# A decoder trunk on one core: first stage with filling products and a dummy activation ahead of x, smaller first pieces, and the sums of squares and small vectors behind the transposed x

## The chip, the core and the metric

The kernel runs on one core of a Trainium2 chip. A core has TensorE (PE, the matrix products; PEld is its weight load), VectorE (DVE), ScalarE (ACT), GpSimd (POOL) and SyncE (SP, which here only issues loads), each with an instruction queue of its own that it works off in order, and sixteen DMA engines that all queues share. Time is device time of one launch in microseconds (us). A profiled execution gives start and length of every instruction.

## What is computed

Two decoder layers on `x` of 256 tokens by 2048 features, float32. Only the head of the first one is touched: an RMS norm, scaled by `mix_norm[0]`, and the product with `conv_w_in` (2048 by 4096).

```python
def rms_norm(x, g):
    y = xf * lax.rsqrt(jnp.mean(xf * xf, axis=-1, keepdims=True) + EPS)
    return y * g
def conv_module(h, w_in, b_in, dw, ...):
    u = h @ w_in + b_in
    a, gate = jnp.split(u, 2, axis=-1)
    v = a * jax.nn.sigmoid(gate)
    v = lax.conv_general_dilated(v, dw[:, None, :], ..., feature_group_count=D_MODEL) + dw_b
    ...
    return v @ w_out + b_out
x = x + conv_module(rms_norm(x, mix_norm[0]), ...)
x = x + mlp(rms_norm(x, mlp_norm[0]), w_up, w_down)
...                                   # second layer: state-space mixer and mlp, then a final norm
```

## The kernel before

Weights are read once from HBM in **steps** of 1 MB, in order (`load`, through `fetch`, on SP's queue; three buffers `raw`). A step is used in two **halves**. For each half `split` makes two matrices: `hi`, the weight rounded by an ACT copy, and `lo`, weight minus `hi`, a subtraction on DVE or, from step 4 on, on POOL (four buffers each). PE then forms hi x hi, hi x lo and lo x hi.

The first product runs over 16 **blocks** of output columns. A block has two steps, so four halves (block 0: halves 0 to 3, block 1: halves 4 to 7, block 2: halves 8 to 11), and a half has 24 products (`mm_g`, L202 to L204) into an `acc` buffer, of which there are two. The right-hand side is the transposed and `mix_norm`-scaled x, `hT`, in 16 feature groups hT0 to hT15, each with a rounded part (ACT, L249) and a rest (DVE, L250), from transposes by PE (L245, tile `xt`), two groups to a PSUM bank.

The norm's factor per token is not applied to x. Sums of squares (`sumsq`: ACT L262 and DVE L259, 128x512 each) give `ss`, `ssm`, then `rstd` by a power on POOL (L277); `bcast_tok` makes two diagonal matrices `dg` from it (DVE L284, ACT L285), and a product with ones (`bc`, L287) spreads it over the partitions, copied to `bcs` (L291). `gate` then multiplies a finished block's `acc` by `bcs` (DVE L437), takes the sigmoid of one half (ACT `ga`, L438, with a table load ahead of the first) and writes `vT` (DVE L439). Only then is that `acc` buffer free: block 2 waits for the gate of block 0. A depthwise convolution of 31 taps on DVE (`cv`, L816) follows each gate.

Small vectors (biases, norms) and the depthwise weights `conv_dw` are loaded on POOL's queue into `dwr` and transposed by PE: `vt` (L338) and sixteen `dwt` (L344); DVE copies them to `vecs` (L340), which `ga` needs, and `dw` (L346).

The order on every engine is set at build time by a list scheduler that runs the program through its own model of durations; `high_priority` moves instructions ahead, and `behind(ins)` (`issue_after`) holds an instruction back until `ins` has been placed. On the chip each engine keeps to that order whatever happens.

Of the kernel before, what the change touches and what calls it, by code (L numbers as in the profile page):

```python
# [9 lines left out]
F32 = mybir.dt.float32  # L10
F32R = mybir.dt.float32r
I32 = mybir.dt.int32
AF = mybir.ActivationFunctionType
ALU = mybir.AluOpType
# [4 lines left out]
P = 128  # L19
# [3 lines left out]
KB = D // P  # L23
NB = T // P
NS = D // 512
# [8 lines left out]
URGENT = 300  # L34


class Trunk:
# [52 lines left out]
        with self.behind(self.fetched) if self.fetched is not None else nullcontext():  # L90
            self.fetched = self.nc.sync.dma_start(out=out, in_=in_)  # L91

    def load(self, i, half=None):
        view, shape, _, _ = self.steps[i]
        for kind in self.before_load.pop(i, ()):
            self.table(*kind)
        if not half:
            self.raws[i] = self.w.tile(shape, F32, tag="raw", name="raw", bufs=3)
        raw = self.raws[i]
        nk = shape[1] // 2  # L100
        k = slice(0, shape[1]) if half is None else slice(half * nk, half * nk + nk)
        if len(shape) == 4:
            for j in range(shape[2]):
                self.fetch(raw[:, k, j, :], view[:, k, j, :])
        else:
            self.fetch(raw[:, k], view[:, k])
        self.loaded = i + 1

    def split(self, h, urgent=True):
        i, half = divmod(h, 2)  # L110
        raw = self.raws[i] if half == 0 else self.raws.pop(i)
        nk = raw.shape[1] // 2
        sl = raw[:, half * nk:(half + 1) * nk]
        hi = self.w.tile([P, nk] + list(raw.shape[2:]), F32R, tag="hi", name="hi", bufs=4)
        lo = self.w.tile([P, nk] + list(raw.shape[2:]), F32R, tag="lo", name="lo", bufs=4)
        with self.tc.high_priority(offset=URGENT if urgent else 0):
            self.nc.scalar.activation(hi, sl, AF.Copy)  # L117
            eng = self.nc.gpsimd if i in self.pool_lo else self.nc.vector
            ins = eng.tensor_tensor(out=lo, in0=sl, in1=hi.bitcast(F32), op=ALU.subtract)  # L119
            if i in self.pool_lo:  # L120
                self.pool_ins = ins
            else:
                self.lo_ins = ins
        self.parts[h] = (hi, lo)
        return ins
# [112 lines left out]
    def to_features(self, src, g, k0, n):  # L238

        nc = self.nc  # L240
        for k in range(k0, k0 + n, 2):
            ps = self.bank([P, 2, T], name="xt")
            for kk in range(2):
                for b in range(NB):
                    nc.tensor.transpose(ps[:, kk, b * P:(b + 1) * P], src[:, b, (k + kk) * P:(k + kk + 1) * P], self.ident)  # L245
            for kk in range(2):
                gk = g[:, k + kk:k + kk + 1]
                h = self.hT(k + kk)
                nc.scalar.activation(h[:, 0, :], ps[:, kk, :], AF.Copy, scale=gk)  # L249
                nc.vector.scalar_tensor_tensor(out=h[:, 1, :], in0=ps[:, kk, :], scalar=gk,  # L250
                                               in1=h[:, 0, :].bitcast(F32), op0=ALU.mult, op1=ALU.subtract)

    def sumsq(self, ssq, n, both=False):

# [40 lines left out]
    def setup(self):  # L295

        nc, a, const = self.nc, self.a, self.const
        m0 = self.small.tile([KB, P], F32, tag="dg", name="m0")
        nc.scalar.dma_start(out=m0, in_=a["mix_norm"][0].rearrange("(k p) -> k p", p=P))
        self.x = const.tile([P, NB, D], F32, name="x")  # L300
        xv = a["x"][0].rearrange("(b p) c -> p b c", p=P)
        for n in range(NS):
            s = slice(n * 512, (n + 1) * 512)
            self.fetch(self.x[:, :, s], xv[:, :, s])
            self.load(n // 2, n % 2)
        self.ident = const.tile([P, P], F32, name="ident")
        make_identity(nc, self.ident)
        self.ones = const.tile([P, P], F32, name="ones")
        nc.vector.memset(self.ones, 1.0)
        self.mhalf = const.tile([P, NB], F32, name="mhalf")  # L310
        nc.vector.memset(self.mhalf, -0.5)
        self.mix0 = const.tile([P, KB], F32, name="mix0")
        ps = self.bank([P, KB], name="mt")
        nc.tensor.transpose(ps, m0, self.ident[0:KB, 0:KB])
        nc.vector.tensor_copy(out=self.mix0, in_=ps)
        self.new_hT()
        ssq = self.new_ssq()
        for n in range(NS):
            self.to_features(self.x, self.mix0, 4 * n, 4)
        for n in range(NS):  # L320
            self.sumsq(ssq, n, True)
        self.rstdB = self.bcast_tok(self.rstd_tok(ssq))
        dwr = self.blk_tile([P, D + P], name="dwr")
        rows, dwr = dwr[:, D:], dwr[0:TAPS, 0:D]
        self.vcol = {}
        r = 0
        for name, ap in (("b_in", a["conv_b_in"][0]), ("dw_b", a["conv_dw_b"][0]),
                         ("ln_g", a["conv_ln_g"][0]), ("ln_b", a["conv_ln_b"][0]),
                         ("mlp0", a["mlp_norm"][0]), ("mlp1", a["mlp_norm"][1])):
            n = ap.shape[0] // P  # L330
            with self.behind(self.pow_ins):
                nc.gpsimd.dma_start(out=rows[r:r + n, :], in_=ap.rearrange("(k p) -> k p", p=P))
            self.vcol[name] = (r, n)
            r += n
        with self.behind(self.pow_ins):
            nc.gpsimd.dma_start(out=dwr, in_=a["conv_dw"][0])
        ps = self.bank([P, 512], name="vt")
        nc.tensor.transpose(ps[:, 0:r], rows[0:r, :], self.ident[0:r, 0:r])  # L338
        self.vecs = const.tile([P, P], F32, name="vecs")
        nc.vector.tensor_copy(out=self.vecs[:, 0:r], in_=ps[:, 0:r])  # L340
        self.dw = const.tile([P, KB, 32], F32, name="dw")
        ps = self.bank([P, KB, 32], name="dwt")
        for k in range(KB):
            nc.tensor.transpose(ps[:, k, 0:TAPS], dwr[:, k * P:(k + 1) * P], self.ident[0:TAPS, 0:TAPS])  # L344
        nc.vector.memset(self.dw[:, :, TAPS:32], 0.0)
        nc.vector.tensor_copy(out=self.dw[:, :, 0:TAPS], in_=ps[:, :, 0:TAPS])  # L346
        self.m32 = const.tile([P, 32], F32, name="m32")
        nc.vector.tensor_reduce(out=self.m32, in_=self.ident.rearrange("p (q c) -> p c q", c=32), axis=AX, op=ALU.add)
        self.q4 = const.tile([P, P], F32, name="q4")
        nc.vector.memset(self.q4, 0.0)  # L350
        for q in range(4):
            nc.vector.memset(self.q4[32 * q:32 * q + 1, :], 1.0)
        self.vT2 = [self.blk_tile([P, 8, VW], name="vT") for _ in range(2)]
        for v in self.vT2:
            nc.gpsimd.memset(v[:, :, 0:PAD], 0.0)
            nc.gpsimd.memset(v[:, :, PAD + T:VW], 0.0)
# [766 lines left out]
    def ssm_slice(self, n):  # L1123
# [13 lines left out]
        def loads(load=self.fetch):  # L1137
            for q in range(NQ):
                c0 = n * 512 + q * P
                load(out=self.xJ[32 * q:32 * q + 32, n], in_=rows[:, :, c0:c0 + P])  # L1140
# [411 lines left out]
```

## Time and profile before

| | us |
|---|---|
| three runs, median (lowest to highest) | 2002.31 (2000.91 to 2003.06) |
| profiled execution, its own time | 2002.3 |
| its span, first to last instruction | 2000.5 |
| PE busy in the span | 1973.6 (99%) |
| first x load issued, first landed | 0.75, 5.05 |
| first product of block 0 starts | 7.95 |
| first product of block 2 starts | 38.58 |

A row of the timeline gives start, length, engine, line, operation, output and inputs, count, and in brackets how long the engine had been idle before it and what ended that. A row with a count merges neighbours. Products follow each other faster than one lasts (they are pipelined), so the pace of PE is read from start to start. Rows with SPq or POOLq are DMA issues; "to landing" is from issue to the last byte.

### The profile page before, as it was taken

The numbers are of one execution on the slowest core, as the hardware profiler recorded it, in microseconds if no ns is written. First come the engines' busy times: TensorE is split into PE (matmuls) and PEld (weight loads), VectorE is DVE, ScalarE is ACT, GpSimd is POOL, SyncE is SP. The second block draws the span as 40 slices with busy tenths as digits, with TensorE's granted clock in tenths as the row PEclk, the third lists the DMA queues.
The fourth block names the chain that finished last, engine by engine and source line by source line (L and its number), as shares of the span: only waits on it lengthen the run. The fifth ranks groups of instructions, "written<-read, shape, count | busy, mean of one in ns | idle before, by whom it ended". The sixth has DMA issues, their size and how long they took to land.

```text
span 2000.5 us, 28951 instructions
## 1 busy us (share of the span) xinstructions
PE 1973.6 (99%) x11626; PEld 1691.4 (85%) x11626; DVE 1400.7 (70%) x1905; ACT 951.4 (48%) x1172; POOL 280.7 (14%) x257
## 2 busy tenths in 40 slices
PE   8999999999999999999999999999999999999998
PEld 8999787888888888888887788888888888888887
DVE  7899899967777778776557756566556555555655
ACT  6444654454444545444444445454444454444444
POOL 3998301000000221222011000000000000000000
PEclk9999999999999999999999999999999999999999
DMA  8768458766865877877897865665656556575653
GB/s 230 189 178 219 134 192 272 237 215 191 266 190 188 220 222 253 267 254 223 319 310 265 315 211 185 190 188 189 191 190 193 189 188 201 185 221 184 195 189 127
DMA packets 317030, 428.49 MB, mean 214 GB/s; under 512 B 9761, under 2 KB 211553, under 8 KB 313537
## 3 DMA queue, kind: packets, MB, share of 16 engines
q1 hardware_dynamic: 301120, 384.85, 60.8%
q0 software_dynamic: 12352, 37.49, 6.3%
q10 hardware_dynamic: 3424, 4.30, 0.8%
q8 instruction: 91, 1.49, 0.3%
q14 instruction: 43, 0.35, 0.0%
HBM read 400.08 MB, written 34.91 MB: 217 GB/s over the span
## 4 chain that ended last, share of the span: by engine, by line
PE 92%; DVE 3%; DMA 2%; issue 1%; SPq 1%; POOL 0%; ACT 0%; ACTq 0%; POOLq 0%; DVEq 0%
PE acc L190 23%; PE acc L213 15%; PE acc L215 15%; PE acc L214 15%; PE acc L193 12%; PE acc L203 3%; PE acc L202 3%; PE acc L204 3%; DVE lo L119 1%; PE pk L475 1%; DMA raw<-in_conv_w_in_dram 1%; SPq L91 1%; DMA Vt<-Vd 0%; PE kp L1100 0%; DMA xs<-x 0%
## 5 line engine op out<-in xcount | busy, mean ns | idle before, releaser
L117 ACT ACTIVATE hi<-raw 128x1024 fp32r<-128x1024 f32 x672 | 712.1, 1061 | 967.1 <-PE acc L215 525.5
L119 DVE TENSOR_TENSOR lo<-raw,hi 128x1024 fp32r<-128x1024 f32 x612 | 748.7, 1225 | 514.9 <-ACT hi L117 513.2
L190 PE MATMUL acc<-hT,hi 128*128 128x512 f32 x2048 | 514.3, 393 | 3.3 <-DVE t L795 3.0
L190 PEld LDWEIGHTS acc<-hT,hi 128*128 128x128 f32 x2048 | 368.8, 189 | 71.8 <-DVE t L795 2.4
L213 PE MATMUL acc<-hi,rT 128*128 128x512 f32 x992 | 387.4, 391 | 0.0
L214 PE MATMUL acc<-lo,rT 128*128 128x512 f32 x992 | 386.3, 389 | 0.0
L215 PE MATMUL acc<-hi,rT 128*128 128x512 f32 x992 | 385.9, 389 | 0.0
L193 PEld LDWEIGHTS acc<-hT,lo 128*128 128x128 f32 x2048 | 279.4, 190 | 20.0
L193 PE MATMUL acc<-hT,lo 128*128 128x256 f32 x2048 | 285.9, 282 | 0.0
L213 PEld LDWEIGHTS acc<-hi,rT 128*128 128x128 f32 x992 | 186.2, 188 | 39.7 <-issue 1.8
L215 PEld LDWEIGHTS acc<-hi,rT 128*128 128x128 f32 x992 | 186.2, 188 | 39.1
L214 PEld LDWEIGHTS acc<-lo,rT 128*128 128x128 f32 x992 | 186.3, 188 | 38.0
L119 POOL TENSOR_TENSOR lo<-raw,hi 128x1024 fp32r<-128x1024 f32 x60 | 143.6, 2412 | 31.4 <-ACT hi L117 29.0
L202 PE MATMUL acc<-hT,hi 128*128 128x256 f32 x512 | 145.9, 286 | 1.3 <-ACT hi L117 1.3
L203 PE MATMUL acc<-hT,hi 128*128 128x256 f32 x512 | 145.6, 285 | 0.3 <-DVE hT L250 0.3
L204 PE MATMUL acc<-hT,lo 128*128 128x256 f32 x512 | 145.3, 286 | 0.0
L816 DVE SCALAR_TENSOR_TENSOR cv<-vT,dw,cv 128x256 f32<-128x256 f32 x348 | 141.1, 480 | 2.2 <-ACT cv L518 1.7
L807 DVE TENSOR_TENSOR x<-x,acc 128x1024 f32<-128x1024 f32 (+1 forms) x72 | 83.4, 1161 | 27.2 <-PE acc L215 23.0
L202 PEld LDWEIGHTS acc<-hT,hi 128*128 128x128 f32 x512 | 98.7, 193 | 3.6 <-ACT hi L117 1.9
L213 PE MATMUL acc<-hi,yT 128*128 128x512 f32 x256 | 101.2, 395 | 0.1
L214 PE MATMUL acc<-lo,yT 128*128 128x512 f32 x256 | 99.9, 390 | 0.6 <-DVE lo L119 0.6
L203 PEld LDWEIGHTS acc<-hT,hi 128*128 128x128 f32 x512 | 98.5, 193 | 2.2 <-issue 1.6
(274 smaller groups left out, 1734.5 us busy)
## 6 DMA issues: line engine op xcount, KB each, us to landing
raw<-in_mlp_w_up_dram SPq DMA_DIRECT2D x128, 1024.0 KB, 5.8
raw<-in_mlp_w_down_dram SPq DMA_DIRECT2D x128, 1024.0 KB, 5.1
raw<-in_ssm_w_glu_dram SPq DMA_DIRECT2D x32, 1024.0 KB, 5.6
raw<-in_conv_w_in_dram SPq DMA_DIRECT2D x60, 512.0 KB, 5.6
raw<-in_conv_w_out_dram SPq DMA_DIRECT2D x16, 1024.0 KB, 5.2
Vd<-bv POOLq DMA_DIRECT2D x16, 512.0 KB, 5.0
Md<-Kd POOLq DMA_DIRECT2D x32, 256.0 KB, 8.1
Wt<-Wd SPq DMA_DIRECT2D x8, 1024.0 KB, 8.9
```

The lines of the kernel that those rows point to most:

```text
L117: self.nc.scalar.activation(hi, sl, AF.Copy)
L119: ins = eng.tensor_tensor(out=lo, in0=sl, in1=hi.bitcast(F32), op=ALU.subtract)
L190: mm(accs[m], lhsT=hi[:, kk, cs[m]], rhs=xT(k0 + kk), start=first and kk == 0, stop=False)
L193: mm(accs[m][:, 0:T], lhsT=lo[:, kk, cs[m]], rhs=xT(k0 + kk)[:, 0, :], start=False, stop=last and kk == 3)
L202: mm(accs[m], lhsT=hi[:, kk, c], rhs=x[:, 0, :], start=first and kk == 0, stop=False)
L203: mm(accs[m], lhsT=hi[:, kk, c], rhs=x[:, 1, :], start=False, stop=False)
L204: mm(accs[m], lhsT=lo[:, kk, c], rhs=x[:, 0, :], start=False, stop=last and kk == 3)
L213: mm(acc[:, b, :], lhsT=ak[:, 0, t], rhs=hi[:, kk, :], start=first and kk == 0, stop=False)
L214: mm(acc[:, b, :], lhsT=ak[:, 0, t], rhs=lo[:, kk, :], start=False, stop=False)
L215: self.mm_last = mm(acc[:, b, :], lhsT=ak[:, 1, t], rhs=hi[:, kk, :], start=False, stop=last and kk == 1)
L807: self.nc.vector.tensor_tensor(out=out, in0=a, in1=b, op=op)
L816: return self.nc.vector.scalar_tensor_tensor(out=out, in0=a, scalar=s, in1=b, op0=op0, op1=op1)
```

## The change

Loads: the first quarter of x (512 features) and the first half of the first weight step are fetched in two pieces each, interleaved (x, weights, x, weights), and half 0 is split in two pieces of 512 columns. Ahead of x stand eight products of ones into an unused `acc` buffer (`warm`), and three more behind each of the first two transposes' banks; an ACT Square on one element of ones stands ahead of everything on ACT. The copy of `mix_norm` to `mix0` gets a high priority, and `lo` stands behind it. All sums of squares stand behind the last hT pair. The small vectors' loads stand behind a one-element POOL copy `go` of the last hT group, and no more behind the power.

```diff
-    def load(self, i, half=None):
+    def load(self, i, half=None, part=None):
...
+        if part is not None:
+            k = slice(part * nk // 2, (part + 1) * nk // 2)
...
+        n = nk // 2 if h == 0 else nk
         with self.tc.high_priority(offset=URGENT if urgent else 0):
-            self.nc.scalar.activation(hi, sl, AF.Copy)
             eng = self.nc.gpsimd if i in self.pool_lo else self.nc.vector
-            ins = eng.tensor_tensor(out=lo, in0=sl, in1=hi.bitcast(F32), op=ALU.subtract)
+            for k in (slice(k, k + n) for k in range(0, nk, n)):
+                self.nc.scalar.activation(hi[:, k], sl[:, k], AF.Copy)
+                with self.behind(self.ready):
+                    ins = eng.tensor_tensor(out=lo[:, k], in0=sl[:, k], in1=hi[:, k].bitcast(F32), op=ALU.subtract)
...
         for n in range(NS):
+            if n == 0:
+                for p in range(2):
+                    s = slice(p * 256, (p + 1) * 256)
+                    self.fetch(self.x[:, :, s], xv[:, :, s])
+                    self.load(0, 0, p)
+                continue
...
+        nc.scalar.activation(self.small.tile([P, 1], F32, tag="ld", name="ld"), self.ones[:, 0:1], AF.Square)
+        warm = self.acc2("warm")[:, 0, 0:P]
+        for _ in range(8):
+            nc.tensor.matmul(warm, lhsT=self.ones, rhs=self.ones, start=True, stop=True)
...
-        nc.vector.tensor_copy(out=self.mix0, in_=ps)
+        with self.tc.high_priority(offset=2 * URGENT):
+            self.ready = nc.vector.tensor_copy(out=self.mix0, in_=ps)
...
-        for n in range(NS):
-            self.to_features(self.x, self.mix0, 4 * n, 4)
-        for n in range(NS):
-            self.sumsq(ssq, n, True)
+        for k in (0, 2):
+            ins = self.to_features(self.x, self.mix0, k, 2)
+            self.keep_warm(3, self.xt, warm)
+        for n in range(1, NS):
+            ins = self.to_features(self.x, self.mix0, 4 * n, 4)
+        with self.behind(ins[0]), self.behind(ins[1]):
+            for n in range(NS):
+                self.sumsq(ssq, n, True)
         self.rstdB = self.bcast_tok(self.rstd_tok(ssq))
         dwr = self.blk_tile([P, D + P], name="dwr")
+        go = nc.gpsimd.tensor_copy(out=self.small.tile([P, 1], F32, tag="go", name="go", bufs=1),
+                                   in_=self.hT(KB - 1)[:, 0, 0:1].bitcast(F32))
...
-            with self.behind(self.pow_ins):
+            with self.behind(go):
                 nc.gpsimd.dma_start(out=rows[r:r + n, :], in_=ap.rearrange("(k p) -> k p", p=P))
...
-        with self.behind(self.pow_ins):
+        with self.behind(go):
             nc.gpsimd.dma_start(out=dwr, in_=a["conv_dw"][0])
```

The changed kernel's lines are some 5 to 24 higher than the old ones (L207 to L209 are the products, L122 and L124 the split).

PE before, where the factor is spread over the partitions: `acc_282` is block 0, `acc_438` block 1, and 81 of these two blocks' 192 products stand ahead of `bc`.

```order
L203 MATMUL acc_282<-hT_109,hi_278 128x256
L204 MATMUL acc_282<-hT_109,lo_279 128x256
L202 MATMUL acc_282<-hT_109,hi_278 128x256
L287 MATMUL bc_208<-dg_205,ones_100 128x256
L204 MATMUL acc_438<-hT_108,lo_308 128x256
L202 MATMUL acc_438<-hT_108,hi_307 128x256
L203 MATMUL acc_438<-hT_108,hi_307 128x256
```

PE after, the same place: `acc_462` is block 1, `acc_617` block 2.

```order
L207 MATMUL acc_462<-hT_123,hi_458 128x256
L208 MATMUL acc_462<-hT_123,hi_458 128x256
L209 MATMUL acc_462<-hT_123,lo_459 128x256
L294 MATMUL bc_228<-dg_225,ones_103 128x256
L362 MATMUL vt_242<-ident_98,dwr_232 128x112
L368 MATMUL dwt_247<-ident_98,dwr_232 128x31 x16
L207 MATMUL acc_617<-hT_122,hi_487 128x256
```

`bc`, `vt` and `dwt`, which stood behind 81, 144 and 149 of the 192 products, now all stand behind the 192nd, right ahead of block 2.

ACT before, from the first weights of block 1 (`hi_307`, half 4) to the first sigmoid: `hi_463` and `hi_494` are halves 8 and 9.

```order
L117 ACTIVATE hi_307<-raw_260 128x1024
L117 ACTIVATE hi_338<-raw_260 128x1024
L249 ACTIVATE hT_109<-xt_165,mix0_104 128x256
L285 ACTIVATE dg_205<-ident_95,rstd_203 128x128
L249 ACTIVATE hT_109<-xt_174,mix0_104 128x256
L117 ACTIVATE hi_366<-raw_263 128x1024
L117 ACTIVATE hi_434<-raw_263 128x1024
L117 ACTIVATE hi_463<-raw_335 128x1024
L117 ACTIVATE hi_494<-raw_335 128x1024
L438 ACT_TABLE_LOAD
L438 ACTIVATE ga_394<-acc_282,vecs_222 128x256
```

ACT after, from half 6 (`hi_390`) on: `junk` are squares, `hi_458` is half 7, `hi_487` and `hi_518` (step 4) halves 8 and 9, `hi_546` and `hi_613` (step 5) halves 10 and 11.

```order
L122 ACTIVATE hi_390<-raw_285 128x1024
L269 ACTIVATE junk_211,ssq_124<-x_80 128x512
L269 ACTIVATE junk_215,ssq_124<-x_80 128x512
L122 ACTIVATE hi_458<-raw_285 128x1024
L122 ACTIVATE hi_487<-raw_359 128x1024
L122 ACTIVATE hi_518<-raw_359 128x1024
L122 ACTIVATE hi_546<-raw_455 128x1024
L292 ACTIVATE dg_225<-ident_98,rstd_223 128x128
L122 ACTIVATE hi_613<-raw_455 128x1024
L462 ACT_TABLE_LOAD
L462 ACTIVATE ga_418<-acc_306,vecs_244 128x256
```

`dg` stood behind half 5 and now stands behind half 10, and the table load and the first sigmoid stand behind half 11.

POOL after, from the last of the small loads on: the six loads ahead of it stand behind `go`, which reads hT15.

```order
L360 DMA dwr_232<-in_conv_dw_dram 31x2048
L379 MEMSET vT_274 128x8x30
L380 MEMSET vT_274 128x8x2
L379 MEMSET vT_275 128x8x30
L380 MEMSET vT_275 128x8x2
L124 TENSOR_TENSOR lo_488<-raw_359,hi_487 128x1024
L284 TENSOR_TENSOR rstd_223<-ssm_221,mhalf_116 128x2
L124 TENSOR_TENSOR lo_519<-raw_359,hi_518 128x1024
```

`rstd` was POOL's first work after the identity, ahead of the loads; it now stands behind them and behind `lo` of half 8.

More of the change, by code (lines that the diff above doesn't have):

```diff
@@ L96, in load @@
             self.table(*kind)
-        if not half:
+        if not (half or part):
             self.raws[i] = self.w.tile(shape, F32, tag="raw", name="raw", bufs=3)
@@ L244, in to_features @@
                 for b in range(NB):
-                    nc.tensor.transpose(ps[:, kk, b * P:(b + 1) * P], src[:, b, (k + kk) * P:(k + kk + 1) * P], self.ident)
+                    self.xt = nc.tensor.transpose(ps[:, kk, b * P:(b + 1) * P], src[:, b, (k + kk) * P:(k + kk + 1) * P],
+                                                  self.ident)
             for kk in range(2):
@@ L248, in to_features @@
                 h = self.hT(k + kk)
-                nc.scalar.activation(h[:, 0, :], ps[:, kk, :], AF.Copy, scale=gk)
-                nc.vector.scalar_tensor_tensor(out=h[:, 1, :], in0=ps[:, kk, :], scalar=gk,
-                                               in1=h[:, 0, :].bitcast(F32), op0=ALU.mult, op1=ALU.subtract)
+                hi = nc.scalar.activation(h[:, 0, :], ps[:, kk, :], AF.Copy, scale=gk)
+                lo = nc.vector.scalar_tensor_tensor(out=h[:, 1, :], in0=ps[:, kk, :], scalar=gk,
+                                                    in1=h[:, 0, :].bitcast(F32), op0=ALU.mult, op1=ALU.subtract)
+        return hi, lo
     def sumsq(self, ssq, n, both=False):
```

## The prediction

> **What bounds the kernel now.** I read the page's busy shares first, then busy time by stretch, then the timeline of the first 40 us engine by engine, and the loads' landing times.
>
> ```profile
> PE 1973.6 (99%) x11626; PEld 1691.4 (85%) x11626; DVE 1400.7 (70%) x1905; ACT 951.4 (48%) x1172; POOL 280.7 (14%) x257
> ...
> 0.00:40.00 40.00, 33.91 (x256) 32.57 (x257) 27.12 (x63) 26.81 (x54) 10.40 (x20) 1.00 1.02 264
> 40.00:100.00 60.00, 60.00 (x489) 58.23 (x488) 50.85 (x125) 27.38 (x33) 54.14 (x24) 1.00 0.64 173
> ```
>
> PE is the bound. It is idle for 6.1 of the first 40 us and for none of the next 60. So the change is worth what it does to one moment: when block 2 starts, for from there PE is dense, with the same products to do. PE's rows up to it:
>
> ```profile
> 8.69 1.97 PE L245 MATMUL xt<-ident,x 128*128 128x128 f32 x8
> 11.95 0.41 PE L202 MATMUL acc<-hT,hi 128*128 128x256 f32 x1
> 12.16 0.41 PE L203 MATMUL acc<-hT,hi 128*128 128x256 f32 x1
> 12.91 0.28 PE L202 MATMUL acc<-hT,hi 128*128 128x256 f32 x1
> 13.03 0.28 PE L203 MATMUL acc<-hT,hi 128*128 128x256 f32 x1
> ...
> 15.92 0.60 PE L245 MATMUL xt<-ident,x 128*128 128x128 f32 x4
> 16.28 0.36 PE L203 MATMUL acc<-hT,hi 128*128 128x256 f32 x1
> ...
> 20.15 0.39 PE L203 MATMUL acc<-hT,hi 128*128 128x256 f32 x1 [0.33 <-DVE hT L250]
> ...
> 38.58 0.28 PE L202 MATMUL acc<-hT,hi 128*128 128x256 f32 x1
> ```
>
> Products start 0.21 us apart up to 12.16 and 0.12 apart from 12.9 on, though the granted clock's column reads 1.00 throughout; transposes take 0.2 each early (8 in 1.97) and 0.09 later (4 in the 0.36 from 15.92 to 16.28). PE is dense from 20.15; the last row is the 193rd product, block 2's first.
>
> **What the early part can win.** The weights' landing bounds it. ACT's rows that waited for loads:
>
> ```profile
> 16.92 1.06 ACT L117 ACTIVATE hi<-raw 128x1024 fp32r<-128x1024 f32 x1 [0.44 <-DMA raw<-in_conv_w_in_dram]
> ...
> 20.56 2.01 ACT L117 ACTIVATE hi<-raw 128x1024 fp32r<-128x1024 f32 x2 [1.12 <-DMA raw<-in_conv_w_in_dram]
> ...
> 24.92 1.06 ACT L117 ACTIVATE hi<-raw 128x1024 fp32r<-128x1024 f32 x1 [1.34 <-DMA raw<-in_conv_w_in_dram]
> ...
> 30.02 1.06 ACT L117 ACTIVATE hi<-raw 128x1024 fp32r<-128x1024 f32 x1 [2.37 <-DMA raw<-in_conv_w_in_dram]
> ```
>
> Half 3 landed at 16.9, step 2 at 20.5, step 3 at 24.9, step 4 at 30.0; the DMA share of the first 40 us is 1.02, so the loads are saturated, and smaller pieces change the order of the first bytes, not when a later step is in. SP's three more issues come out of that queueing; I price them at 0.
>
> In the new order PE does 92 products (all but six of block 0, and two of block 1), and the 93rd waits for `lo` of half 4:
>
> ```profile
> 21.65 2.36 DVE L119 TENSOR_TENSOR lo<-raw,hi 128x1024 fp32r<-128x1024 f32 x2 [0.58 <-ACT hi L117]
> ```
>
> That is 21.65 and half of 2.36, so 22.8, set by step 2's landing. PE gets there in time: once x's second quarter is in (8.69) 86 of the 92 and 24 transposes remain, 10.3 and 2.2 us at the quick pace, so 21.2; if the pace stays slow until 12.4, as before, some 1.8 later, 23.0. So what a quicker clock saves is waited away here but for 0.2; I price the fourteen fillers at 0, and the cover is this wait. From 22.9, 100 products by 0.12: PE is through block 1 at 34.9. Before, the 192 were done at 38.58 with some 1.8 of `bc`, `vt` and `dwt` among them, so at 36.8 by the same measure: **the early part wins 1.9 us.** Squares moved out of ACT and DVE (about 2.5 us of each before 17) feed this and win nothing more. The early copy to `mix0` lets the first hT go without the squares ahead of it, part of the same. The dummy Square replaces a table load that no one waited for: 0. Two half-size splits for one cost ACT some 0.2, ahead of loads: 0.
>
> **What the late part costs.** `bc` now stands behind product 192, and block 2's first product behind block 0's gate, which follows `bc`. Nothing covers that chain any more. First, when `bc` can run. The rows:
>
> ```profile
> 15.40 0.63 ACT L262 ACTIVATE junk<-x 128x512 f32<-128x512 f32 x1
> 9.07 0.69 DVE L259 SCALAR_TENSOR_TENSOR junk<-x 128x512 f32<-128x512 f32 x1
> 31.16 4.73 POOL L119 TENSOR_TENSOR lo<-raw,hi 128x1024 fp32r<-128x1024 f32 x2 [6.40 <-ACT hi L117]
> 19.79 0.72 POOL L277 TENSOR_TENSOR rstd<-ssm,mhalf 128x2 f32<-128x2 f32 x1 [18.48 <-DVE ssm L275]
> 22.83 0.39 ACT L285 ACTIVATE dg<-ident,rstd 128x128 f32<-128x128 f32 x1
> ...
> 20.13 2.80 SPq L91 DMA_DIRECT2D raw<-in_conv_w_in_dram  x1
> DMA to landing us min/median/max: 9.8/9.8/9.8
> 24.75 1.86 SPq L91 DMA_DIRECT2D raw<-in_conv_w_in_dram  x1
> DMA to landing us min/median/max: 8.7/9.2/9.7
> 23.58 0.53 POOL L336 DMA_DIRECT2D dwr<-in_conv_dw_dram  x1
> dwr<-in_conv_dw_dram POOLq DMA_DIRECT2D x1, 248.0 KB, 7.6
> ```
>
> DVE's squares stand behind hT15 (`lo` of half 5 ends at 24.0, plus 0.4) with `lo` of halves 6 and 7 between them, so with half 7's `hi` at 28.3 (step 3, two copies, two squares) `ssm` is there at about 29.8. But POOL's `rstd` is behind `lo` of half 8, which needs step 4 (30.0), 1.06 for `hi` and 2.4 for `lo`: 33.5, and 0.72: 34.2. And ACT's `dg` is behind `hi` of half 10, which needs step 5. Its second part was issued at 24.75 (its buffer comes free with `lo` of half 5, at 24.0 in both) and took up to 9.7: 34.4. So `hi` ends at 35.5 and `dg` at 35.9. Waiting behind `dg` on ACT: `hi` of half 11, table load, `ga`.
>
> Step 5's landing is the unknown. The small loads now start behind ACT's hT15 (20.56 + 2.01 for two copies + 0.4 = 23.0) and not behind `rstd` (20.5), so `conv_dw`, issued at 23.58 before, goes out near 26.5, a little `go` included. Early end: none of its 248 KB is ahead of step 5, which at 264 GB/s is 0.9, so 33.5. Late end: as before, 34.4. I take the middle, 33.9, as either row is equally near; `hi` then ends at 35.0 and `dg` at 35.4, half a microsecond after PE is through block 1. So `bc` runs at 35.4; the ends are 34.9 (product 192) and 35.9.
>
> From `bc` to block 2:
>
> ```profile
> 23.45 0.59 PE L287 MATMUL bc<-dg,ones 128*128 128x256 f32 x2
> 27.16 0.42 DVE L291 COPY bcs<-bc 128x256 f32<-128x256 f32 x1
> 31.73 0.28 DVE L340 COPY vecs<-vt 128x112 f32<-128x112 f32 x1 [1.27 <-PE vt L338]
> 39.18 0.69 DVE L437 TENSOR_TENSOR acc<-acc,bcs 128x512 f32<-128x512 f32 x1
> 34.79 0.67 DVE L346 COPY dw<-dwt 128x496 f32<-128x496 f32 x1
> 34.39 0.48 DVE L439 SCALAR_TENSOR_TENSOR vT<-acc,vecs,ga 128x256 f32<-128x256 f32 x1 [2.39 <-ACT ga L438]
> 32.59 1.28 ACT L438 ACT_TABLE_LOAD   x1
> 33.88 0.48 ACT L438 ACTIVATE ga<-acc,vecs 128x256 f32<-128x256 f32 x1
> 32.22 1.18 PE L344 MATMUL dwt<-ident,dwr 31*128 31x31 f32 x16
> ```
>
> DVE's new order is `bcs`, `vecs`, both blocks' multiplications, `dw`, then `vT`: 0.59 + 0.42 + 0.28 + 2 x 0.65 + 0.67 + 0.48 = 3.7. ACT's branch, 1.06 + 1.28 + 0.48 = 2.8, is covered by it. PE has 1.8 of work in those 3.7 (the last row's `dwt` most of it), so it stands still for 0.5 ahead of `bc` and 1.9 behind it. Block 2 starts at 35.4 + 3.7 = 39.1, against 38.58: the late part costs 2.4 and the early part won 1.9, **net +0.5 us**. Bounds: 34.9 gives 0.0, 35.9 gives +1.0.
>
> Behind block 2 the products are the same. DVE's depthwise chain begins later, behind both gates, and is some four taps of 0.4 behind where it stood; it catches up in these waits for PE, 5.6 us, which hide it. Without them it would cost at most those 1.6:
>
> ```profile
> 86.33 0.70 DVE L437 TENSOR_TENSOR acc<-acc,bcs 128x512 f32<-128x512 f32 x1 [2.16 <-PE acc L204]
> ...
> 98.58 0.70 DVE L437 TENSOR_TENSOR acc<-acc,bcs 128x512 f32<-128x512 f32 x1 [3.45 <-PE acc L204]
> ```
>
> The sum is made against the profiled execution's own 2002.3 us, which is the median of the three runs (2000.91 to 2003.06): 2002.3 + 0.5 = **2002.8 us**. About 0.2% (4 us) is what a measurement of this kernel can tell from no change.
>
> **The rivals.** *The clock's saving comes through.* Before, 16 transposes and 11 products ran at the slow pace; at the quick one they would take 16 x 0.11 + 11 x 0.09 = 2.8 us less, so 1999.5 if nothing were waited for behind them. For it: the pace did change at 12.4. Against it: product 93 waits for a load that lands when it did, and `bc` for two more; it needs step 2 some 2 us earlier, and the chain behind `bc` short. [...]
>
> *Fillers that don't warm.* If the pace still changes near 12.4, block 1 ends 0.2 later, and `bc` still waits for `dg`: 2002.8 again.
>
> *Step 5 comes late (the slower side).* `conv_dw` has a queue of its own. The second part of step 4 flew beside it and took 9.8. If step 5 got half of the rate for all 7.6 us of that load on top of its 9.7, it would land at 24.75 + 9.7 + 3.8 = 38.3; then `hi`, `dg` and 3.7 more: 43.4, so +4.9 and 2007.2. It is slower by over 4 us from a landing at 37.4 on. Against it: the same bytes passed before step 5's end in both. [...]
>
> **How the numbers follow.** Block 2 set by the chain behind `bc`, 2002.0 to 2003.6: 0.60, and the prediction. Clock's saving through, in part or whole, 1999.5 to 2002.0: 0.22. Step 5 late, 2003.6 to 2007.2: 0.12, half of it above 2006.3. Order changes further down that I priced at 0: 0.06, half beyond 4 us on the good side and half on the bad. So faster 0.04, slower 0.09, the same 0.87. The range drops a tenth at each side: 1999.8 to 2005.0.
>
> **What would show it.** Right: PE's `bc` behind product 192 at 35 to 36 after a wait for `dg`, then PE idle for about 2 us with `vT` named as releaser, block 2 at 38.6 to 39.6; `dg` on ACT directly behind `hi` of half 10. Wrong: block 2 before 37.5 (the early part came through), `dg` long before product 192, or a step 5 past 37. The clock step: 0.12 spacing by 9 to 10 us if the fillers warm.

## The result, and the profile after

| | before | changed |
|---|---|---|
| five runs each, median (lowest to highest) | 2002.0 (2000.03 to 2003.06) | 2008.91 (2008.68 to 2012.43) |
| ratio | | 1.0044, interval 1.0033 to 1.0055 |
| profiled execution, its own time and span | 2002.3, 2000.5 | 2012.43, 2010.7 |
| block 2's first product | 38.58 | 39.89 |

By the medians the change makes the kernel 6.9 us slower; the ratio corresponds to 8.8 us (6.6 to 11.0). The forecast was +0.5, with a range up to 2005.0. The profiled execution is the longest of the five changed ones; the three near 2008.8 have a mean granted clock of 0.997 or 0.998, this one 0.996.

In the changed kernel lines have moved: L202 to L204 are L207 to L209, `xt` is L250, hT L255 and L256, `hi` L122, `lo` L124, `bc` L294, `dg` on ACT L292, `ga` L462, `vT` L463. First the page's busy shares, then busy time in the second of the stretches that the prediction showed (PE, PEld, DVE, ACT, POOL, then the granted clock, the DMA share and GB/s):

```profile
PE 1979.8 (98%) x11654; PEld 1696.1 (84%) x11654; DVE 1402.0 (70%) x1906; ACT 951.6 (47%) x1174; POOL 282.1 (14%) x258
```
```profile
40.00:100.00 60.00, 60.00 (x476) 58.37 (x477) 52.57 (x129) 27.47 (x42) 47.74 (x22) 0.97 0.61 165
```

From 40 to 100 us PE is as busy as before, but its granted clock is 0.97 where it was 1.00. PE's timeline shows the place:

```profile
8.20 0.28 PE L208 MATMUL acc<-hT,hi 128*128 128x256 f32 x1
8.32 0.28 PE L209 MATMUL acc<-hT,lo 128*128 128x256 f32 x1
...
9.74 1.09 PE L250 MATMUL xt<-ident,x 128*128 128x128 f32 x8 [0.78 <-DMA x<-in_x_dram]
...
24.29 0.39 PE L209 MATMUL acc<-hT,lo 128*128 128x256 f32 x1 [0.24 <-DVE lo L124]
...
36.38 0.60 PE L294 MATMUL bc<-dg,ones 128*128 128x256 f32 x2
...
37.01 1.18 PE L368 MATMUL dwt<-ident,dwr 31*128 31x31 f32 x16
39.89 0.39 PE L207 MATMUL acc<-hT,hi 128*128 128x256 f32 x1 [1.70 <-DVE vT L463]
...
40.98 0.42 PE L209 MATMUL acc<-hT,lo 128*128 128x256 f32 x1
41.20 0.41 PE L207 MATMUL acc<-hT,hi 128*128 128x256 f32 x1
...
44.19 0.34 PE L209 MATMUL acc<-hT,lo 128*128 128x256 f32 x1
44.36 0.28 PE L207 MATMUL acc<-hT,hi 128*128 128x256 f32 x1
```

The fillers do warm, with eight transposes among them: products are 0.12 apart at once, from 8.2 us (12.9 before, 15.2 in the change without fillers, e4). Product 93, the first that needs `lo` of half 4, runs at 24.29 and not at the forecast 22.8. Two things are late there by nearly the same amount. `lo` is (below), but PE waits for it only 0.24, for it is through product 92 only at 24.05, where the prediction had 21.2: x's second quarter is in at 9.74 (8.69 before), and the 86 products and 24 transposes that remain then take 14.3 us and not 12.5. `bc` comes directly behind product 192 at 36.38; `vT` releases block 2 after 3.5 us. Then something new: from 40.98 to 44.19 products are 0.21 apart again, at a granted clock of 0.50 (41 to 44 us). Those are fifteen steps of 0.21 for 0.12, 1.4 us, and a little at either end: some 1.5 us lost behind the gap.

Why half 4 is late, in the busy times of the first loads (granted clock, DMA share, GB/s; the kernel before, then the changed one) and ACT's row for step 2:

```profile
0.00:4.00 4.00, 1.00 0.38 109
4.00:8.00 4.00, 1.00 1.03 322
```
```profile
0.00:4.00 4.00, 1.00 0.48 137
4.00:8.00 4.00, 1.00 0.81 230
```
```profile
21.91 2.01 ACT L122 ACTIVATE hi<-raw 128x1024 fp32r<-128x1024 f32 x2 [1.87 <-DMA raw<-in_conv_w_in_dram]
```

With the smaller pieces the DMA engines are not full between 4 and 8 us: by 8 us they had moved 109 x 4 + 322 x 4 = 1724 KB before and 1468 KB now. The missing 256 KB are 0.8 us at 322 GB/s, and step 2 is in at 21.91, where it was 20.56. What made up the other 0.5 us isn't shown.

The late start is 1.3 us at block 2 and, with the half-speed stretch, 2.4 us by the last of the sixteen blocks (DVE multiplies its `acc` at 217.42, and at 215.02 before). Most of the loss is elsewhere. The profiled ends differ by 10.2 us (spans of 2010.7 and 2000.5). The table products `u8t` and `ct`, which both kernels issue in the first MLP, bracket it:

```profile
352.15 0.57 PE L1005 MATMUL u8t<-ident,u 128*64 128x64 f32 x12
...
638.07 0.60 PE L1066 MATMUL ct<-ident,cr 128*128 128x128 f32 x4
```
```profile
354.39 0.57 PE L1029 MATMUL u8t<-ident,u 128*64 128x64 f32 x12
...
647.98 0.71 PE L1090 MATMUL ct<-ident,cr 128*128 128x128 f32 x5
```

At `u8t` the changed kernel is 2.2 us late, at `ct` 9.9. In between stand all of PE's waits (in total, times, longest; before, then changed) that the profile puts to `t`:

```profile
PE acc L190 <- DVE t L795: 3.0, 2, 2.1
```
```profile
PE acc L195 <- DVE t L819: 7.8, 4, 3.5
```

The waits for `lo` are the same in both, 2.9 us in all, and lie outside this stretch (near 310 and 1125 us).

`t` is the first operation of the MLP's squared relu (`relu2`): it reads a finished `acc` and so frees the buffer for PE. DVE has other work there: the state-space layer of the second half of the program needs tables (W, in stages of three operations on 128x1024, 1.13 us from start to start: `wt`, `ws`), which are computed in the background from 300 us on. DVE's rows ahead of the fourth `t`, before and changed:

```profile
388.50 0.68 DVE L229 TENSOR_TENSOR rT<-u,rT 128x512 fp32r<-128x512 f32 x1
389.10 0.68 DVE L795 TENSOR_TENSOR t<-acc,t 128x512 f32<-128x512 f32 x1
```
```profile
392.46 0.68 DVE L234 TENSOR_TENSOR rT<-u,rT 128x512 fp32r<-128x512 f32 x1
393.07 1.21 DVE L831 TENSOR_TENSOR ws<-bb,pw 128x1024 f32<-128x1024 f32 x1
394.20 1.22 DVE L831 TENSOR_TENSOR wt<-bb,pw 128x1024 f32<-128x1024 f32 x1
395.34 1.21 DVE L124 TENSOR_TENSOR lo<-raw,hi 128x1024 fp32r<-128x1024 f32 x1
396.47 0.21 DVE L831 TENSOR_TENSOR pw<-pw,wk 128x64 f32<-128x64 f32 x1
396.61 0.68 DVE L819 TENSOR_TENSOR t<-acc,t 128x512 f32<-128x512 f32 x1
```

Before, `t` stands right behind `rT`; now two table operations, a `lo` and a small one stand between, 3.5 us, and PE waits 3.49 for that `t`. Nothing in the change names these lines. The number of `wt`/`ws` operations that the built program has on DVE ahead of the first six `t`:

```
before   24 29 31 37 41 42
changed  23 29 34 40 42 42
```

And PE's granted clock behind that wait (PE busy, clock, DMA share, GB/s of the changed kernel):

```profile
396.00:400.00 4.00, 2.56 (x6) 0.50 0.62 195
400.00:404.00 4.00, 4.00 (x17) 0.66 0.75 211
```

So between `u8t` and `ct` the loss of 7.7 us is 4.8 of waits, and the 2.9 that are left are about what PE lost at half speed, in and behind the longest of them.

### The profile page after: what moved, and what is told of

It is laid out like the page before. It is cut to its first block, busy times and chain, and to the rows that moved or that the text cites. A ratio compares the mean times of both kernels' runs of the same rounds, so it can differ in the third digit from the quotient of the medians.

```text
span 2010.7 us, 29013 instructions
## 1 busy us (share of the span) xinstructions
PE 1979.8 (98%) x11654; PEld 1696.1 (84%) x11654; DVE 1402.0 (70%) x1906; ACT 951.6 (47%) x1174; POOL 282.1 (14%) x258
## 4 chain that ended last, share of the span: by engine, by line
PE 90%; DVE 5%; DMA 1%; issue 1%; SPq 1%; ACT 0%; POOL 0%; ACTq 0%; POOLq 0%; DVEq 0%
PE acc L195 22%; PE acc L218 15%; PE acc L219 15%; PE acc L220 15%; PE acc L198 11%; PE acc L209 3%; PE acc L207 3%; PE acc L208 3%; DVE lo L124 2%; PE pk L499 1%; SPq L91 1%; DVE ws L831 1%; DVE wt L831 1%; DMA Vt<-Vd 0%; PE kp L1124 0%
## 5 line engine op out<-in xcount | busy, mean ns | idle before, releaser
L122 ACT ACTIVATE hi<-raw 128x1024 fp32r<-128x1024 f32 (+1 forms) x673 | 712.7, 1059 | 980.8 <-PE acc L220 519.1
L124 DVE TENSOR_TENSOR lo<-raw,hi 128x1024 fp32r<-128x1024 f32 (+1 forms) x613 | 747.8, 1221 | 525.3 <-ACT hi L122 522.3
L195 PEld LDWEIGHTS acc<-hT,hi 128*128 128x128 f32 x2048 | 369.9, 189 | 77.9 <-issue 8.2
L198 PEld LDWEIGHTS acc<-hT,lo 128*128 128x128 f32 x2048 | 280.2, 191 | 20.1
L220 PEld LDWEIGHTS acc<-hi,rT 128*128 128x128 f32 x992 | 186.2, 188 | 39.1
L207 PE MATMUL acc<-hT,hi 128*128 128x256 f32 x512 | 145.9, 286 | 1.7 <-DVE vT L463 1.7
L124 POOL TENSOR_TENSOR lo<-raw,hi 128x1024 fp32r<-128x1024 f32 x60 | 143.6, 2408 | 28.1 <-ACT hi L122 28.0
L209 PE MATMUL acc<-hT,lo 128*128 128x256 f32 x512 | 145.5, 286 | 0.4 <-DVE lo L124 0.2
L207 PEld LDWEIGHTS acc<-hT,hi 128*128 128x128 f32 x512 | 98.8, 193 | 3.1 <-DVE vT L463 1.8
L209 PEld LDWEIGHTS acc<-hT,lo 128*128 128x128 f32 x512 | 98.5, 193 | 2.6 <-issue 1.2
```

Of the source, the lines that this page charges most:

```text
L122: self.nc.scalar.activation(hi[:, k], sl[:, k], AF.Copy)
L124: ins = eng.tensor_tensor(out=lo[:, k], in0=sl[:, k], in1=hi[:, k].bitcast(F32), op=ALU.subtract)
L195: mm(accs[m], lhsT=hi[:, kk, cs[m]], rhs=xT(k0 + kk), start=first and kk == 0, stop=False)
L198: mm(accs[m][:, 0:T], lhsT=lo[:, kk, cs[m]], rhs=xT(k0 + kk)[:, 0, :], start=False, stop=last and kk == 3)
L207: mm(accs[m], lhsT=hi[:, kk, c], rhs=x[:, 0, :], start=first and kk == 0, stop=False)
L209: mm(accs[m], lhsT=lo[:, kk, c], rhs=x[:, 0, :], start=False, stop=last and kk == 3)
```

## The experiments

Theory 1: two places, the start (2 to 3 us) and a changed order of DVE's table work in the first MLP (the rest). Theory 2: the start costs everything. All ratios are to the kernel before, timed on the same chip. The forecasts in us were made against 2002.0; on the chips of the experiments the kernel before took 2000.33 to 2000.43, so a forecast is better compared as a ratio.

**e1, the change with the old table counts.** The table operations from number 32, 38 and 42 on are placed behind the third, fourth and fifth `t`.

```diff
-        nc.vector.tensor_tensor(out=t, in0=acc[:, :, 0:T], in1=t, op=ALU.add)
+        self.adds.append(nc.vector.tensor_tensor(out=t, in0=acc[:, :, 0:T], in1=t, op=ALU.add))
...
+            def tt(*q):
+                self.big += 1
+                k = [k for n, k in ((32, 3), (38, 4), (42, 5)) if self.big >= n]
+                with self.behind(self.adds[k[-1] - 1]) if k else nullcontext():
+                    h(*q)
```

> The changed kernel, with one thing added: from the first MLP's third sum `t` on, VectorE gets as many of the SSM table operations ahead of each `t` as in the kernel before (31, 37, 41 and 42 ahead of the third to sixth, where the change had 34, 40, 42 and 42). Everything ahead of the first MLP is as in the change. Theory 1 (two places: the start costs some 2.5 us, and a changed order of VectorE's work in the first MLP the rest): TensorE's waits for `t` fall from 7.8 back to about 3.0 us, no half-speed stretch near 400 us, and the time is 2004.5 (2003.5 to 2005.5). Theory 2 (the start costs everything, and the waits for `t` only sit where others would come up): 2008 to 2009.

Measured: 2006.21 (2004.91 to 2008.48), ratio 1.0029 (1.0017 to 1.0040).

```profile
PE acc L196 <- DVE t L820: 3.4, 3, 1.3
```

The waits fell as theory 1 said, and the long one with its half-speed stretch is gone, but the time did not follow: theory 1's range is 1.0007 to 1.0017 of 2002.0, theory 2's 1.0030 to 1.0035, and 1.0029 is next to the second. Its trace has half-speed stretches behind other waits (at 40, 313 and 357 us). The old counts undo a part of the loss at most; the interval overlaps that of the change. This run alone doesn't decide.

**e2, the change with the loads as before; e3, the kernel before with fillers only; e4, the change without fillers.**

```diff
# e2
-        n = nk // 2 if h == 0 else nk
+        n = nk
...
-            if n == 0:
-                for p in range(2):
...
# e4
-        for _ in range(8):
-            nc.tensor.matmul(warm, lhsT=self.ones, rhs=self.ones, start=True, stop=True)
...
-            self.keep_warm(3, self.xt, warm)
# e3, put into the kernel before
+        nc.scalar.activation(self.small.tile([P, 1], F32, tag="ld", name="ld"), self.ones[:, 0:1], AF.Square)
+        warm = self.acc2("warm")[:, 0, 0:P]
+        for _ in range(8):
+            nc.tensor.matmul(warm, lhsT=self.ones, rhs=self.ones, start=True, stop=True)
```

> The changed kernel with the first loads in pieces of the old size (x in four, the first weight step in two halves) and one split for the first half; fillers, dummy activation, late squares and late vectors stay. VectorE's order in the first MLP is then that of the kernel before, without being asked for. Theory 1: loads land 1 us earlier than in the change, so TensorE is through block 1 at about 35.2 and block 2 starts at 38.5 to 39; a slow stretch behind it may stay (1.5 us); waits for `t` about 3.0; 2002 to 2004. Theory 2: the late squares and vectors are still there, so most of the loss stays: 2006 to 2008.

Measured: 2003.95 (2001.94 to 2005.60), 1.0014 (1.0005 to 1.0023). Step 2 is in at 20.27, yet `bc` runs at 36.16, as in the change: the first product starts 1.3 us later (9.35), and PE then has few gaps. So the pieces give at the first product what they take at step 2. Block 2 is as late as in the change (39.66), the half-speed stretch is there, and with the waits for `t` at 2.1 it is 5 to 8 us quicker than the two timings of the change (the second is e11). The ratio lies between the two forecasts (1.0000 to 1.0010 and 1.0020 to 1.0030); what speaks against theory 2 is that the start is as late as the change's and the interval is clear of the change's.

> The kernel before with only the eight filling products and the dummy activation ahead of x. `bc`, `vt` and `dwt` stay inside block 1. VectorE's order in the first MLP comes out as in the change (34 and 40 tables ahead of the third and fourth `t`). Theory 1: the start gains 0 to 1 us, the order costs 4 to 5, with a slow stretch or without: 2005 to 2007. Theory 2: nothing of the start is late, so 2001 to 2002.5.

Measured: 2011.41 (2009.16 to 2016.41), 1.0058 (1.0045 to 1.0071).

```profile
PE acc L190 <- DVE t L799: 6.1, 3, 3.5
```

Neither range holds it. Eight fillers alone did not bring the quick pace: products are still 0.21 apart at 11.8 us, about as in the kernel before. `bc` and `vt` are inside block 1, and the last block's multiplication is 1.3 us late (216.27); `ct` is 8.8 us late. A kernel with eight products more at its start, and the start's squares and vectors in their old places, loses as much as the whole change, and most of it in the first MLP: `u8t` is 1.3 us late. Theory 2, that the start costs everything, falls.

> The changed kernel without its fourteen filling products; the order of everything else in the first MLP is the same as in the change. If the fillers buy the quick pace from 7 us on and nothing takes it back: 2 to 3 us slower than the change, 2011 to 2012. If the load waits take it back, as the prediction said: within 0.5 us of the change, 2008.5 to 2009.5, with the 0.12 spacing only from about 12 us on.

Measured: 2011.66 (2010.61 to 2013.66), 1.0057 (1.0044 to 1.0069).

```profile
14.96 0.42 PE L209 MATMUL acc<-hT,lo 128*128 128x256 f32 x1
15.18 0.33 PE L207 MATMUL acc<-hT,hi 128*128 128x256 f32 x1
15.35 0.28 PE L208 MATMUL acc<-hT,hi 128*128 128x256 f32 x1
```

Without fillers the quick pace begins at 15.2 us, and block 2 starts at 41.16 (39.89 in the change): the fillers are worth 1.3 us there. The time fits the first forecast, but the intervals of this run and of the change overlap.

**e5, e1 with the gap filled; e6, the change with the squares early.**

```diff
# e5
+            last = nc.tensor.transpose(ps[:, k, 0:TAPS], dwr[:, k * P:(k + 1) * P], self.ident[0:TAPS, 0:TAPS])
+        self.keep_warm(14, last)
# e6
-        with self.behind(ins[0]), self.behind(ins[1]):
-            for n in range(NS):
-                self.sumsq(ssq, n, True)
+        for n in range(NS):
+            self.sumsq(ssq, n, True)
```

> Run e1 (the change with the old number of table operations ahead of each `t`) and fourteen more filling products of 128 columns on TensorE behind the last `dwt`, so that TensorE is busy in the 1.7 us in which it stood still ahead of block 2. Block 2 itself still waits for `vT`. If the half-speed stretch behind block 2's start (products 0.21 apart for 3.4 us in the change and in every run with that gap) comes from the low activity ahead of it: no such stretch, block 2 where it was (39.6 to 39.9), 1.6 us less than e1, so 1.0021 of the kernel before. If it comes from something else (the loads, the two heavy blocks before): the stretch stays and the time is e1's 1.0029 or a little more.

Measured: 2005.96 (2003.58 to 2006.85), 1.0025 (1.0014 to 1.0035).

```profile
38.35 3.39 PE L187 MATMUL warm<-ident 128*128 128x128 f32 x28
41.50 0.36 PE L208 MATMUL acc<-hT,hi 128*128 128x256 f32 x1
41.70 0.28 PE L209 MATMUL acc<-hT,hi 128*128 128x256 f32 x1
```

From 41.70 on products are 0.12 apart, and the stretch is gone. But the fillers were too many, 0.23 each, and held block 2 back from 39.6 to 41.5, by a little more than the stretch had cost. In time the run is inconclusive.

> The changed kernel with the sums of squares back in their old place (not behind the last hT); the vectors stay behind `go`. `bc` then stands behind product 78 and `vt`, `dwt` behind 184 and 190, all inside block 1, and VectorE's order in the first MLP falls back to that of the kernel before (31 and 37 tables ahead of the third and fourth `t`). Theory 1: block 2 starts at 38 to 38.8 with a wait below 0.7 and no slow stretch; waits for `t` about 3; 0.999 to 1.001 of the kernel before. Theory 2, that the early part itself (loads 1 us later, pieces, fillers) costs: 1.0015 or more.

Measured: 2005.54 (2003.87 to 2009.32), 1.0025 (1.0015 to 1.0035). Theory 1 missed it, and the number is one that theory 2 allowed (1.0015 or more). But the trace doesn't put the loss at the start: that is as theory 1 said (block 1's multiplication on DVE at 39.41, 39.18 before; no gap, no stretch), the last block's is 0.9 us late (215.95), and the waits for `t` are 3.0. A wait came up in a third place, at the end of the convolution, and a half-speed stretch 9 us behind it:

```profile
PE pk L498 <- DVE R L484: 2.9, 1, 2.9
```

**e7 and e8, tables held.** Each table stage is placed behind the last `t` ahead of it in the program, in the kernel before (e7) and in the change (e8); `adds` collects the `t` as in e1.

```diff
-            self.cmul_half(i, ws[:, :, i, :], (w0[:, :, 0, :], w0[:, :, 1, :]), pw, t)
+            with self.behind(self.adds[-1]) if self.adds else nullcontext():
+                self.cmul_half(i, ws[:, :, i, :], (w0[:, :, 0, :], w0[:, :, 1, :]), pw, t)
```

> The kernel before, with each W table stage of the SSM (three operations of 1.13 us on VectorE) kept behind the last `t` that stands ahead of it in the program: 6, 6, 9, 12 table operations ahead of the first four `t`, where it had 24, 29, 31, 37. Nothing else is touched. If VectorE's table work is what TensorE waits for there: waits for `t` go from 3.0 to 0 to 0.5 us, and with them a slow stretch in some executions: 0.998 to 0.9987. If the waits only move (to `lo`, or to the SSM, which needs the tables later): 0.999 to 1.000.

> The changed kernel with the same hold as in e7. Theory 1: waits for `t` from 7.8 to 0 to 0.5, no half-speed stretch near 400; what is left is the start (block 2 1.3 late and 1.6 for the slow stretch behind it), against 3.0 us of waits that the kernel before has: 0.999 to 1.0008. Theory 2 (the start costs it all): 1.003.

Measured: e7 1992.35 (1992.25 to 1994.10), 0.9962 (0.9948 to 0.9975); e8 1994.53 (1993.05 to 1999.39), 0.9974 (0.9964 to 0.9984). e7 is the quickest of all runs, 8 us below the kernel before; e8 is 14 below the change. Both did better than their forecasts. DVE's busy time from 300 to 400 us shows why, in the kernel before and in e7:

```profile
300.00:350.00 50.00, 50.00 (x69) 0.97 0.86 272
350.00:400.00 50.00, 50.00 (x69) 1.00 0.80 238
```
```profile
300.00:350.00 50.00, 41.95 (x78) 1.00 0.82 255
350.00:400.00 50.00, 41.96 (x48) 1.00 0.69 210
```

In the kernel before DVE never stops in these 100 us; it is the bound there, under an average of 70%. With the tables held it has 8 us free in each 50 (the table work comes later: DVE is busy for 45.2 of the next 50 us, where it was for 34.3), and PE is busy all of 300 to 450 us (97.0 of the 100 from 350 on before, 91.6 in the change). Besides the waits for `t` those for `lo` near 310 went (2.9 to 0.6 in all), which the forecast for e7 had not counted; so it gained 7.6 us and not 3 to 4. In the profiled executions, which are 10.0 us apart, 8.2 are gained by `ct` (629.90); the rest lies between 1060 and 1120 us, where PE waits 2.2 us for `xJ` in the kernel before, with a half-speed stretch (granted clock 0.50 from 1075 to 1077 us), and 0.8 in e7, with none. No run takes that place apart. No half-speed stretch remains in the traces of e7 and e8 before the last 7 us of the program. From the end of the convolution on (213 us) DVE's operations stand in the same order in both, and then the change costs 2.2 us in the medians, with intervals that overlap. That is what is left for the start.

**e9 to e12.** With the tables held: the early part alone (e9: late squares undone as in e6, vectors behind `pow_ins`), the late part alone (e10: only these lines, put into the kernel before), and e8 with seven fillers behind the last `dwt` (e12). e11 is the change again, on their chip.

> The early part alone, with the tables held as in e7 and e8 so that VectorE's order from the first MLP on is the same in all of them: fillers, dummy activation, small first pieces, early `mix0`; squares in their old place and the vectors behind `rstd`, so `bc` stands behind product 78 and `vt`, `dwt` behind 158 and 163. If the early part wins the 1.9 us that the prediction gave it: 0.9953 of the kernel before (e7 had 0.9962). If the loads' landing 1.0 to 1.35 us later takes most of it, as the trace of the change says: block 1 done near 38.2, a gain of about 0.4 us on e7, 0.9960 (0.9953 to 0.9968).

Measured: 1994.58 (1993.18 to 1994.75), 0.9965 (0.9951 to 0.9978). PE around `bc`:

```profile
22.15 0.60 PE L295 MATMUL bc<-dg,ones 128*128 128x256 f32 x2
24.41 0.39 PE L208 MATMUL acc<-hT,hi 128*128 128x256 f32 x1 [1.67 <-ACT hi L123]
...
25.67 0.38 PE L210 MATMUL acc<-hT,lo 128*128 128x256 f32 x1 [0.75 <-DVE lo L125]
```

The ratio lies in the second range, but not for the reason given there. Step 2 is in only at 23.30 (21.91 in the change), PE stands still for 2.4 us until it is split, and block 1's multiplication on DVE is at 40.84 (39.14 in e7), not earlier; why the load is later still isn't shown. The early part alone wins nothing that can be told; the 1.9 us of the prediction are not there.

> The late part alone, with the tables held: loads, splits and clock as in the kernel before, squares behind the last hT and the small vectors behind `go`, so `bc`, `vt` and `dwt` stand behind product 192. PE through block 1 at 36.8, then 3.5 us from `bc` to block 2: block 2 near 40.3, so 1.7 us later than e7, and 1.6 more in executions with a slow stretch behind the gap: 0.9970 to 0.9979 of the kernel before. If the late part costs nothing of its own: 0.9962.

Measured: 1996.53 (1994.77 to 1998.10), 0.9978 (0.9970 to 0.9987), as expected.

```profile
36.68 0.60 PE L289 MATMUL bc<-dg,ones 128*128 128x256 f32 x2
...
40.18 0.38 PE L203 MATMUL acc<-hT,hi 128*128 128x256 f32 x1 [1.70 <-DVE vT L444]
...
41.70 0.42 PE L205 MATMUL acc<-hT,lo 128*128 128x256 f32 x1
```

Block 2 is 1.6 us later than in the kernel before, and a half-speed stretch follows (granted clock 0.66 over 40 to 45 us). By the last block it is 4.3 us behind e7 (218.73, 214.46), so some 1 us more than the two account for.

> The changed kernel as it is, timed beside the others. Theory 1 (its own start 2 to 3 us, a worse order of VectorE's table work in the first MLP the rest): 1.0035 to 1.0055 as before, and 14 us (0.007) above e8.

Measured: 2011.99 (2008.22 to 2014.03), 1.0052 (1.0040 to 1.0065): 0.0078 above e8.

> Run e8 (the change with tables held) with seven filling products behind the last `dwt`; in e5 one took 0.23 us, so they fill 1.6 of the 1.7 us in which TensorE waits for `vT`. If that gap is what brings the half-speed stretch in some executions: block 2 where it was (39.7), no slow stretch behind it, and the times bunch at e8's low end (1993 to 1994.5), 0.9963 to 0.9968. If the stretch has another cause: 0.9974 and a spread to 1999, as in e8.

Measured: 1996.06 (1994.38 to 1996.31), 0.9972 (0.9962 to 0.9983).

```profile
37.90 1.83 PE L187 MATMUL warm<-ident 128*128 128x128 f32 x14
39.63 0.39 PE L208 MATMUL acc<-hT,hi 128*128 128x256 f32 x1
39.85 0.28 PE L209 MATMUL acc<-hT,hi 128*128 128x256 f32 x1
```
```profile
PE stat L556 <- DVE vT L842: 1.7, 1, 1.7
```

Half right: the gap is filled to the point, block 2 starts where it did, at full pace, and the spread is 2 us, not 6. But the time is e8's, whose own profiled execution had the gap and no stretch. DVE's order changed once more, and at the end of the convolution PE waits 1.7 us for `vT` (the last row, from the list of its waits).

## Why the prediction was wrong

- **"Order changes further down that I priced at 0: 0.06"** is the step that failed most: it was priced at nothing, and `ct` came 7.7 us later against `u8t` than before. Holding the same table work back is worth 8 us in the kernel before (e7) and 14 to 16 in the change (e8 against both timings of the change), and what differs there, 300 us behind the changed lines, is its place in DVE's order. The prediction took "the products are the same" for "the order is the same". That the builder's order follows its model of durations, so that any edit at the start may move it, is argued from e2 and e6, which fell back to the old counts, and e3, which got the change's from the third `t` on by fillers alone; no run shows the builder's reasons. Nor do the counts alone settle it: e1 has the old ones and still took 1.0029.
- **"Smaller pieces change the order of the first bytes, not when a later step is in"** failed: step 2 landed 1.35 us later. The DMA share of 1.02 over 40 us hid that it can fall to 0.81 from 4 to 8 us. Put into the prediction's own sum (22.8 + 1.35, 100 products by 0.12, 3.5 for the chain) it gives 39.7, against 39.89 measured, but that fit is partly luck, because the next step failed too.
- **"PE gets there in time ... so 21.2"** failed by as much: PE was through product 92 at 24.05. By these rows product 93 would have run only 0.24 us earlier with step 2 on time. Of the 2.85 us, 1.05 are x's second quarter, which landed later as well, and 1.8 are products and transposes that took 14.3 us and not 12.5, 0.7 of it a wait for hT. The early part won 0.4 us (36.8 to 36.38) and not 1.9.
- **"I price the fourteen fillers at 0"** was mis-sized: 1.3 us at block 2 (e4). Its bound, a slow pace until 12.4 as before, was too kind; with the changed start the slow pace lasts to 15.2.
- **"From `bc` to block 2 ... 3.7"** was right: 3.5, in the order given, with `vT` as releaser and PE idle for 1.7. Step 5 was not late (ACT's `hi` of half 10 began at 33.64, the early end of the forecast), so that rival did not happen. Its half rate beside `conv_dw` is shown by no run: in the changed kernel step 5's second part, issued at 25.8, took 7.7 us to landing, where that sum had 9.7 + 3.8, with `conv_dw` (issued at 28.47, 6.4 to landing) beside it. The wait for `dg` ahead of `bc` didn't happen either: product 192 came last. It was close, for DVE's half of `dg` took 2.42 us and ended at 36.04, 0.34 ahead of `bc`; the prediction had priced ACT's half alone.
- **"Behind block 2 the products are the same"** was right in number and wrong in pace: 1.5 us for the half-speed stretch behind the gap, in six of the seven traces that have the gap unfilled.

The sum, then: the start is 2.4 us by the last block (gap, stretch, loads and PE's late arrival together), and the rest is DVE's order, with the half-speed stretches behind the waits that it makes. On the start alone the forecast was 0.8 us off (39.1 against 39.89).

## What to carry to other kernels

Where a scheduler sets the order, an edit moves instructions far from its lines: compare the whole built order of every engine, and put a price on each stretch where another engine is busy without a break. Such a stretch is found in windows, not in the average (DVE at 70% over the program, and at 100% from 300 to 400 us). Background work that may wait should be tied behind the work that frees a buffer: here that alone is worth 0.4%, more than the change had set out to move.

## What the runs showed of the hardware that was not expected

A wait of PE was often followed by a stretch of half granted clock, and then cost more than its length. Counted over the fourteen traces, from 30 to 1200 us, by the granted clock: a wait of PE of 1.6 to 2.4 us was followed by such a stretch in 17 of 30 cases, one of 3.5 us in all four. Behind the one of 2.9 us (e6) the stretch came 9 us later, and three more stretches stand behind waits of 1.0 to 1.3. In the changed kernel PE waited 1.70 us ahead of block 2; the stretch behind block 2's start lasted 3.4 us (40.98 to 44.36, granted clock 0.50 from 41 to 44) and cost 1.5 more. The small `vt` and `dwt` transposes ran just ahead of that wait; ahead of others no such transposes ran. Why one wait has a stretch behind it and another has none isn't shown.

Two small operations of DVE became long beside POOL. In the changed kernel `ssm` and DVE's `dg` took 2.18 and 2.42 us, where they took 0.16 and 0.28 before, and each ended within 0.1 us of POOL's `lo` that ran beside it (30.09 to 32.74 for `ssm`, 33.56 to 35.95 for `dg`):

```profile
33.62 2.42 DVE L291 TENSOR_SCALAR dg<-ident,rstd 128x128 f32<-128x128 f32 x1 [0.85 <-POOL rstd L284]
```

In all nine traces with late squares `dg` ran beside such a `lo` and took 2.42 to 2.44 us; in the five others it ran beside none and took 0.28. DVE's multiply-adds of the convolution did not slow down beside the same `lo` (0.48 us either way).

Of the loads: in the changed kernel an issue on SP's queue took about 0.5 us up to 5.3 us (0.47 for the piece of x at 2.25), and with pieces of 128 to 256 KB at the head the rate from 4 to 8 us was 230 and not 322 GB/s. It was not for want of issued loads: one of 512 KB, issued at 3.79, was awaited by PE until 9.74. Why the engines were not full isn't shown.
